# DRAM weight sums issued one per job, and 512-wide output products over half the inputs, in a two-layer mLSTM and GLA decoder kernel

## The chip, the cores and the metric

The kernel runs on one core of a Trainium2 chip. The metric is the time of one execution on the device in microseconds (us). Engines are named as in the profile: PE (TensorE matmuls), PEld (its weight loads), DVE (VectorE), ACT (ScalarE), POOL (GpSimd) and SP (SyncE, whose queue issues most DMAs).

## What is computed

Two layers over 512 tokens of width 1024, each `x <- x + RMSNorm(mixer(RMSNorm(x)))`. Layer 0 is an mLSTM mixer, layer 1 a gated linear attention (GLA). The parts that the change touches:

```python
uz = h @ w_in;  u, z = uz[..., :2048], uz[..., 2048:]      # layer 0
uc = silu(causal_conv(u))
q, k = uc_head @ wq, uc_head @ wk;  v = u_head @ wv        # 4 heads of 512
gates = q @ wg_q + k @ wg_k + v @ wg_v + b_gate            # 8 gates per token
hh = mlstm(q, k / sqrt(512), v, log_i, log_f)
y = (headnorm(hh) * norm_w + skip * uc) * silu(z)
out = y @ w_out                                            # 2048 -> 1024
...
v = h1 @ g_w_in[:, 2048:4096]                              # layer 1, the v projection
```

## The kernel before

Everything is float32, and each large product is made of three float32r matmuls: operands are split into a high part (ACT, line 138) and a low part (DVE, line 139), and high times high, high times low and low times high are added up in PSUM. Weights come in chunks of 128 x 1024 (512 KB): SP loads a chunk into one of three `raw` buffers (line 155), ACT makes `whi`, DVE makes `wlo`, in four buffers each.

The program is a list of jobs in a fixed order, most of which consume one chunk. `run_jobs` goes through the list: before a job it splits the chunks of the next three jobs (`LA`), then runs what earlier jobs put off (`later`), then as many entries of `steps` and `spare` as the job names, and then the job itself. Every engine executes its instructions in the order in which this program writes them.

Layer 0 works head by head. For each head there are four u jobs (`u_job`: 24 matmuls 512 wide, then the splitting of u and the convolution on ACT and DVE), two v jobs (`v_job`), two q jobs and two k jobs (`qk_job`). After the first u jobs of heads 1 to 3 the scores of the head before are made. The gate products of v (`v_gate`, lines 395 to 398) are put off in `spare` and made on DVE, POOL and ACT a few per job, from rows of weights (`wv`, line 390) that SP loads; their sum (`v_gates_end`, line 409) feeds the gacc matmuls behind head 3's score. The gate products of q and k are gacc matmuls at line 378, which read an ACT copy of q (line 541).

Layer 1's v projection is a Strassen-like product of 7 instead of 8 blocks, and needs sums of weight blocks. These sums (`vws`: U, W, Z and R, four tiles of 512 KB each) are made in DRAM by DMAs that POOL issues: 16 plain copies (`vws_start`, line 516) and 16 accumulating ones (`vws_add`, line 520). In the kernel before, each q and k job of heads 1 to 3 issues the next three of the 32, as long as there are any. Layer 1 reads the sums at about 690 us.

The output product of layer 0 has eight blocks of 128 features, two halves of the inputs (8 tiles of y each, `c` = 0 and 1; the second one holds heads 2 and 3) and two halves of the tokens. The first `NF` = 3 blocks take their first half of the inputs in `out_full` jobs: one chunk, with the token halves one after the other, 256 wide. Two of these jobs run before the last head's attention, and the third one has the last head's normalisation (`mid`, which is `head_steps`) between its token halves. For the other blocks `out_job` loads the chunk of `c` = 0 once for each token half. Blocks 3 and 4 take their `c` = 0 jobs of half 0 ahead of the second halves of the inputs. All are 256 wide.

When the first job of token half 1 is done, `after_half0` queues the residual step of half 0: the norm's factor, and then six `add` steps with an empty step after each, one step per job. `add` scales block pairs, adds the residual, and splits the result for layer 1 (`x1_done`, lines 927 to 930). The first norm matmul of layer 1 (`pre_rstd`) follows behind the last output job and needs all of them.

Of the kernel before, what the change touches and what calls it, by code (L numbers as in the profile page):

```python
# [9 lines left out]
F32 = mybir.dt.float32  # L10
# [3 lines left out]
ALU = mybir.AluOpType  # L14
AX = mybir.AxisListType

P = 128
# [79 lines left out]
def tile_mlstm_gla(ctx, tc, xT, pvec, cst, wg, wgv, w_min, w_qk, w_v, w_mout,  # L97
                   w_gqk, w_gr, w_gu, w_gv, w_gz, w_gout, pw, lvl_masks, out):
    nc = tc.nc
# [18 lines left out]
    def psum(name):  # L118
        return pp.tile([P, T], F32, tag="ps", bufs=8, name=name)

    def mm(out, lhsT, rhs, start, stop, more=False):

        nc.tensor.matmul(out, lhsT=lhsT, rhs=rhs, start=start, stop=stop, skip_group_check=more)  # L123
# [26 lines left out]
    def later(k, fn):  # L150
        laters.append([k, fn])
# [158 lines left out]
        eng.tensor_add(acc[:, sl], acc[:, sl], sq[:, sl])  # L310
        return acc

    def proj(ps, chunk, rhi, rlo, start=True, stop=True, sl=FULL):
        whi, wlo = chunk
        n = len(rhi)
        for k in range(n):
            wh, wl = part(whi, k * P, P), part(wlo, k * P, P)
            mm(ps, wh, rhi[k][:, sl], start and k == 0, False)
            mm(ps, wh, rlo[k][:, sl], False, False)
            mm(ps, wl, rhi[k][:, sl], False, stop and k == n - 1)  # L320

    def natural(pss, chunk, base, lhi, llo, total):
        whi, wlo = chunk
# [83 lines left out]
    def v_gates_end():  # L407
        for h in range(1, NH):
            nc.vector.tensor_add(vg[:, 0], vg[:, 0], vg[:, h])
        for i in range(4):  # L410
            mm(gacc[0:8, i * P:(i + 1) * P], vg[:, 0, i, :], ident, False, i == 3)

    A = [None] * NH
    V = [None] * NH
    st = {}
# [6 lines left out]
    def u_conv(n, src):  # L422
        c = t2("conv")
        nc.scalar.activation(c, src, AF.Identity, bias=col(PV_CB + n), scale=col(PV_CW + 48 + n))  # L424
        for j in range(1, 4):
            nc.vector.scalar_tensor_tensor(c[:, j:], src[:, 0:T - j], col(PV_CW + 16 * (3 - j) + n),  # L426
                                           c[:, j:], op0=ALU.mult, op1=ALU.add)

        def act():
            uc = t2("uc")  # L430
            use(SILU)
            nc.scalar.activation(uc, c, AF.Silu)
            ch[n], cl[n] = t2("chi", F32R), t2("clo", F32R)
            split(ch[n], cl[n], uc)
            us = t2("us")
            nc.scalar.mul(us, uc, col(PV_SKIP + n))
            nc.sync.dma_start(uc_d[n], us)

        later(1, act)
# [16 lines left out]
    def u_job(n):  # L456
        def run(chunk):
            ps = psum("u")
            if n < 4:
                proj(ps, chunk, ghi, glo)  # L460
                fps.append(ps)
            else:
                proj(ps, chunk, hhi, hlo)
                u_split(n, ps)
                u_conv(n, ps)
            if n == 2:
                acc = None
                for k in range(KD):
                    acc = add_square(acc, xt[k])
                st["accx"] = acc  # L470
            if n == 3:
                st["rsx"] = rstd_of([st["accx"]], D)
                u_scaled(range(4), fps)
                steps.extend([lambda k=k: h_step((k, k + 1)) for k in range(0, KD, 2)])

        job(run, ring(w_min[n]), b=3, la=1 if n == 2 else LA)
# [10 lines left out]
    def v_evac(h, pss):  # L487
        V[h] = t2s(f"V{h}", 4)
        for i in range(4):
            nc.scalar.activation(V[h][i], pss[i], AF.Copy, accum_out=vmean[:, 4 * h + i:4 * h + i + 1])  # L490
        c = vmean[:, 4 * h:4 * h + 4]
        nc.vector.tensor_scalar_mul(c, c, -1.0 / T)
        if h < NH - 1:
            for i in range(4):
                nc.sync.dma_start(v_d[4 * h + i], V[h][i])
        v_gates(h)

    def v_job(h, c):
        def run(chunk):
            if c == 0:  # L500
                st["v"] = [psum("v") for _ in range(4)]
            pss = st["v"]
            natural(pss, chunk, 2 * c, [uh[4 * h + i] for i in range(4)], [ul[4 * h + i] for i in range(4)], 4)
            if c == 1:
                later(1, lambda: v_evac(h, pss))

        job(run, ring(w_v[2 * h + c]), n=1, b=4)

    q32 = {}


    vws = {(n, p, c): dp.tile([P, 1024], F32, name=f"vw{n}{p}{c}") for n in "UWZR" for p in range(2) for c in range(2)}

    def vws_start(n, p, c):
        a11, a12, a21 = w_gv[2 * p, c], w_gv[2 * p, 2 + c], w_gv[2 * p + 1, c]
        nc.gpsimd.dma_start(vws[n, p, c], {"U": a21, "W": a11, "Z": a12, "R": a11}[n])

    def vws_add(n, p, c):
        a21, a22 = w_gv[2 * p + 1, c], w_gv[2 * p + 1, 2 + c]
        nc.gpsimd.dma_start(vws[n, p, c], {"U": a22, "W": vws["U", p, c], "Z": vws["W", p, c], "R": a21}[n],  # L520
                            accum_op=ALU.add, max_dma_last_dim=4096)

    vsums = [lambda n=n, p=p, c=c, f=f: f(n, p, c) for f in (vws_start, vws_add) for n in "URWZ"
             for p in range(2) for c in range(2)]

    def qk_job(h, which, c):
        d = (q, kq)[which]

        def run(chunk):
            whi, wlo = chunk  # L530
            for e in range(2):
                n = 4 * h + 2 * c + e
                ps = psum("qk")
                for k in range(4):
                    wh, wl = part(whi, k * 256 + e * P, P), part(wlo, k * 256 + e * P, P)
                    mm(ps, wh, ch[4 * h + k], k == 0, False)
                    mm(ps, wh, cl[4 * h + k], False, False)
                    mm(ps, wl, ch[4 * h + k], False, k == 3)
                d[n] = t2("qkh", F32R), t2("qkl", F32R)
                q32[n] = t2("q32")  # L540
                nc.scalar.copy(q32[n], ps)
                split(*d[n], ps)

            if c:
                parts = [(wgs[:, 16 * which + n, :], q32.pop(n)) for n in range(4 * h, 4 * h + 4)]
                later(2 if h else 3, lambda: gate_add(parts))
            if h:
                for f in [vsums.pop(0) for _ in range(min(3, len(vsums)))]:
                    f()

        job(run, ring(w_qk[which, 2 * h + c]), n=1, b=(1, 4, 4, 6)[h])

# [18 lines left out]
    def z_job(n=1, b=0, early=False):  # L571
        i = znext[0]
        znext[0] += 1

        def run(chunk):
            ps = psum("z")
            proj(ps, chunk, *((ghi, glo) if early else (hhi, hlo)))

            def evac():
                zs[i] = t2(f"z{i}")  # L580
                if early:
                    nc.vector.tensor_mul(zs[i], ps, st["rsx"])
                else:
                    nc.scalar.copy(zs[i], ps)
                raw_z.append(i)

            later(1, evac)

        job(run, ring(w_min[16 + i]), n=n, b=b)
# [230 lines left out]

    OUT = {}

    NF = 3

    KP = KD // 2

# [4 lines left out]
    def out_full(n, mid=None):  # L831

        def run(chunk):
            for half in range(2):
                OUT["ps", n, half] = psum("op")[:, HALF[half]]
                proj(OUT["ps", n, half], chunk, yhi[0:8], ylo[0:8], True, False, HALF[half])
                if mid and half == 0:
                    mid()

        job(run, ring(w_mout[2 * n]))  # L840

    def out_job(n, c, half, after=None):

        sl = HALF[half]

        def run(chunk):
            r = slice(8 * c, 8 * c + 8)
            if c == 0:
                OUT["ps", n, half] = psum("op")[:, sl]
            ps = OUT["ps", n, half]  # L850
            assert c == 0 or all(yhi[r])
            proj(ps, chunk, yhi[r], ylo[r], c == 0, c == 1, sl)
            if c == 1:
                if n % 2 == 0:
                    OUT["o", half, n // 2] = t2("o")
                OUT["acc", half] = add_square(OUT["acc", half] if n else None, ps, sl)
                nc.scalar.mul(pair(OUT["o", half, n // 2])[:, n % 2, :], ps, col(PV_POST + n))
            if after:
                after()

        job(run, ring(w_mout[2 * n + c]))
# [86 lines left out]
    def after_half0():  # L948
        rstd, add = residual(0)
        steps.append(rstd)  # L950
        for k in range(KP + 2):
            steps.extend([lambda k=k: add(k), lambda: None])

    rstdB, addB = residual(1)

    out_stage(lambda: (head_steps(NH - 1), steps.extend([lambda: None] * 4 + [lambda i=i: gla_weights(i // 2, i % 2) for i in range(4)])),
              after_half0, 2, 2)

# [379 lines left out]
        job(run, ring(w_gz[n]), la=la)  # L1340

    job(lambda: nc.vector.reduce_max(mx, nref, axis=AX.X), n=0)
    gz_job(0)
    job(lambda: (range_test(), gscale(0, 7), gscale(1, 7)))
    gz_job(1)
# [332 lines left out]
```

## Time and profile before

| | |
|---|---|
| median of 3 runs | 910.5 us (909.35 to 911.77) |
| profiled execution | 915.67 us |
| its span in the trace | 914.0 us |
| PE busy in the span | 892.4 us (98%) |
| DVE, ACT, POOL busy | 672.2, 559.9, 208.3 us |
| mean granted clock of PE | 0.994 of full |
| chunk loads for the output product of layer 0 | 29 |

The span is the time from the first to the last recorded instruction of the profiled execution; 1.67 us of that execution lie around it. Busy times count an engine's instructions as the trace has them. Matmuls overlap in PE's pipeline, so that the duration of one is longer than the step from one start to the next.

### The profile page before, as it was taken

To read this page: it belongs to the slowest core of one execution; us is meant where nothing else is said; L and a number is where in the kernel's file an instruction comes from. 1 tells how busy PE (TensorE), PEld (TensorE's weight loads), DVE (VectorE), ACT (ScalarE), POOL (GpSimd) and SP (SyncE) were. 2 spreads that over 40 slices of the span, in tenths; PEclk is the share of its full clock that TensorE was granted. 3 is DMA by queue.
4 is the path that set the end of the run, shared out by engine and by line. 5 is a ranking of instruction groups with operands and counts; after the bars stand their busy time and mean duration, and the time that the engine had idled before them with its cause. 6 is when DMAs were issued, how large, how long until landed. Compare 5 with 4: busy or idle time off the path is not lost. (4 is left out here: it accounts for less than half of the span.)

```text
span 914.0 us, 12691 instructions
## 1 busy us (share of the span) xinstructions
PE 892.4 (98%) x4576; PEld 746.7 (82%) x4576; DVE 672.2 (74%) x978; ACT 559.9 (61%) x953; POOL 208.3 (23%) x211
## 2 busy tenths in 40 slices
PE   9999999999998999999999999999999999999995
PEld 6887876778876788899999998777778888888884
DVE  5899796789796568878758764853786676778974
ACT  6866684775873558756666554546556555655762
POOL 0013563366170031445001130322000001201001
PEclk9999999999999999999999999999999999999998
DMA  8354488479797334223576696798277959976846
GB/s 304 122 171 134 132 278 286 137 231 259 226 221 216 104 127 138 89 74 115 180 225 207 206 292 229 190 245 211 93 257 251 306 185 328 301 268 216 278 142 138
DMA packets 63492, 185.34 MB, mean 203 GB/s; under 512 B 7392, under 2 KB 11872, under 8 KB 62880
## 3 DMA queue, kind: packets, MB, share of 16 engines
q1 hardware_dynamic: 52320, 137.07, 44.9%
q0 software_dynamic: 10816, 47.19, 20.0%
q8 instruction: 37, 0.61, 0.3%
q10 hardware_dynamic: 288, 0.22, 0.1%
q14 instruction: 31, 0.25, 0.1%
HBM read 160.33 MB, written 58.72 MB: 240 GB/s over the span
## 5 line engine op out<-in xcount | busy, mean ns | idle before, releaser
L139 DVE TENSOR_TENSOR wlo<-raw,whi 128x1024 fp32r<-128x1024 f32 (+1 forms) x158 | 205.9, 1314 | 83.4 <-ACT whi L138 82.2
L138 ACT CAST whi<-raw 128x1024 fp32r<-128x1024 f32 (+1 forms) x158 | 162.5, 1040 | 85.6 <-DMA raw<-in_w_min 26.6
L395 POOL TENSOR_TENSOR vp<-V,wv 128x512 f32<-128x512 f32 x56 | 87.4, 1652 | 165.3 <-ACT V L490 86.3
L123 PE MATMUL op<-yhi,whi 128*128 128x256 f32 x256 | 73.5, 287 | 0.0
L123 PE MATMUL op<-yhi,wlo 128*128 128x256 f32 x256 | 72.5, 283 | 0.4 <-DVE wlo L139 0.4
L123 PE MATMUL op<-ylo,whi 128*128 128x256 f32 x256 | 72.8, 284 | 0.0
L398 DVE SCALAR_TENSOR_TENSOR vp<-V,wv 128x512 f32<-128x512 f32 x72 | 69.2, 1000 | 3.2 <-DMA wv<-in_wgv 3.2
L123 PE MATMUL gz<-g2h,whi 128*128 128x512 f32 x128 | 51.2, 400 | 1.1 <-PEq L1301 1.1
L123 PE MATMUL qk<-chi,whi 128*128 128x512 f32 x128 | 50.2, 392 | 0.0
L123 PE MATMUL qk<-clo,whi 128*128 128x512 f32 x128 | 50.0, 390 | 0.2 <-DVE clo L139 0.2
L123 PE MATMUL gz<-g2h,wlo 128*128 128x512 f32 x128 | 50.0, 390 | 0.0
L123 PEld LDWEIGHTS op<-ylo,whi 128*128 128x128 f32 x256 | 49.1, 192 | 1.1 <-DVE ylo L139 0.6
L123 PE MATMUL qk<-chi,wlo 128*128 128x512 f32 x128 | 49.9, 390 | 0.0
L123 PE MATMUL gz<-g2l,whi 128*128 128x512 f32 x128 | 49.8, 389 | 0.0
L123 PEld LDWEIGHTS op<-yhi,wlo 128*128 128x128 f32 x256 | 49.1, 192 | 0.6 <-DVE wlo L139 0.6
L123 PEld LDWEIGHTS op<-yhi,whi 128*128 128x128 f32 x256 | 49.1, 192 | 0.5 <-issue 0.5
L123 PE MATMUL z<-hhi,whi 128*128 128x512 f32 x112 | 44.7, 399 | 0.0
L123 PE MATMUL z<-hlo,whi 128*128 128x512 f32 x112 | 44.4, 397 | 0.0
L123 PE MATMUL z<-hhi,wlo 128*128 128x512 f32 x112 | 44.2, 395 | 0.0
L426 DVE SCALAR_TENSOR_TENSOR conv<-u,pv,conv 128x511 f32<-128x511 f32 (+2 forms) x48 | 35.8, 748 | 11.3 <-ACT conv L424 10.2
L738 POOL TENSOR_TENSOR sq<-sq 128x512 f32<-128x512 f32 x12 | 17.6, 1470 | 108.2 <-ACT sq L736 107.9
L1254 POOL DMA_DIRECT2D gvhi<-gv_d x8 | 4.3, 543 | 147.3 <-DMA wpP<-klo 119.9
(320 smaller groups left out, 2606.6 us busy)
## 6 DMA issues: line engine op xcount, KB each, us to landing
raw<-in_w_min SPq DMA_DIRECT2D x30, 512.0 KB, 4.4
raw<-in_w_mout SPq DMA_DIRECT2D x29, 512.0 KB, 4.1
wv<-in_wgv SPq DMA_DIRECT2D x32, 256.0 KB, 5.8
raw<-in_w_qk SPq DMA_DIRECT2D x16, 512.0 KB, 4.3
raw<-in_w_gqk SPq DMA_DIRECT2D x16, 512.0 KB, 4.0
raw<-in_w_gz SPq DMA_DIRECT2D x16, 512.0 KB, 7.4
raw<-in_w_gv SPq DMA_DIRECT2D x12, 512.0 KB, 4.2
raw<-in_w_v SPq DMA_DIRECT2D x8, 512.0 KB, 7.4
```

The lines of the kernel that those rows point to most:

```text
L123: nc.tensor.matmul(out, lhsT=lhsT, rhs=rhs, start=start, stop=stop, skip_group_check=more)
L138: nc.scalar.copy(hi, src)
L139: nc.vector.tensor_sub(lo, src, hi.bitcast(F32))
L395: nc.gpsimd.tensor_mul(j, V[h][i], w)
L398: nc.vector.scalar_tensor_tensor(j, V[h][i], 1.0, w, op0=ALU.mult, op1=ALU.mult, accum_out=o)
L426: nc.vector.scalar_tensor_tensor(c[:, j:], src[:, 0:T - j], col(PV_CW + 16 * (3 - j) + n), c[:, j:], op0=ALU.mult, op1=ALU.add)
L738: nc.gpsimd.tensor_add(sqs[0], sqs[0], sqs[vt])
L1254: nc.gpsimd.dma_start(VS[h][i][r], gv_d[8 * (h - 2) + 4 * i + r])
```

## The change

The 32 DMAs of the weight sums are issued one at a time: one behind each u job from block 4 on (12), one behind each v job and each q or k job of heads 1 to 3 (6 and 12), and one behind the evacuation of each z job until the list is empty (the last 2). Their definitions move ahead of the u jobs. A line further down fails at build time if any is left.

`NF` becomes 5, and `out_full` makes both token halves at once, with 512-wide matmuls into one PSUM bank; `mid` now runs after the fourth of its eight input tiles. `out_job` for these blocks adds to one half of that bank at a time. The two `c` = 0 jobs of half 0 that ran ahead (`ahead` = 2) are gone, so blocks 0 to 4 each load the chunk of their first half of the inputs once, and the stage has 27 chunks. In `after_half0` the empty steps behind the last four `add` steps are dropped.

```diff
-    def proj(ps, chunk, rhi, rlo, start=True, stop=True, sl=FULL):
+    def proj(ps, chunk, rhi, rlo, start=True, stop=True, sl=FULL, more=False):
...
+    def vsum_next():
+        if vsums:
+            vsums.pop(0)()
...
                 u_split(n, ps)
                 u_conv(n, ps)
+                vsum_next()
...
             if c == 1:
                 later(1, lambda: v_evac(h, pss))
+            if h:
+                vsum_next()
...
             if h:
-                for f in [vsums.pop(0) for _ in range(min(3, len(vsums)))]:
-                    f()
+                vsum_next()
...
                 raw_z.append(i)
+                if not early:
+                    vsum_next()
...
-    NF = 3
+    NF = 5
...
         def run(chunk):
+            ps = psum("op")
             for half in range(2):
-                OUT["ps", n, half] = psum("op")[:, HALF[half]]
-                proj(OUT["ps", n, half], chunk, yhi[0:8], ylo[0:8], True, False, HALF[half])
-                if mid and half == 0:
+                OUT["ps", n, half] = ps[:, HALF[half]]
+            whi, wlo = chunk
+            for k in range(8):
+                wh, wl = part(whi, k * P, P), part(wlo, k * P, P)
+                mm(ps, wh, yhi[k], k == 0, False)
+                mm(ps, wh, ylo[k], False, False)
+                mm(ps, wl, yhi[k], False, k == 7)
+                if mid and k == 3:
                     mid()
...
-            proj(ps, chunk, yhi[r], ylo[r], c == 0, c == 1, sl)
+            proj(ps, chunk, yhi[r], ylo[r], c == 0, c == 1, sl, n < NF)
...
         for k in range(KP + 2):
-            steps.extend([lambda k=k: add(k), lambda: None])
+            steps.extend([lambda k=k: add(k)] + [lambda: None] * (k < 2))
...
-              after_half0, 2, 2)
+              after_half0, 2, 0)
```

## Rows read from the trace of the kernel before

**Rows 1.** The page's busy line: busy us, share of the span, instructions
```profile
PE 892.4 (98%) x4576; PEld 746.7 (82%) x4576; DVE 672.2 (74%) x978; ACT 559.9 (61%) x953; POOL 208.3 (23%) x211
```

**Rows 2.** Windows by stage: us, busy us (instructions) by engine, clock, DMA share, GB/s
```profile
74.74:105.47 30.73, 30.73 (x156) 25.30 (x153) 26.34 (x39) 19.44 (x38) 14.94 (x11) 1.00 0.43 131
105.47:149.12 43.65, 42.33 (x185) 31.68 (x183) 36.17 (x53) 30.29 (x69) 26.27 (x25) 1.00 0.82 274
149.12:185.54 36.42, 35.54 (x170) 29.61 (x169) 25.71 (x40) 24.01 (x50) 8.93 (x6) 1.00 0.48 161
...
215.78:250.75 34.97, 34.97 (x172) 29.75 (x169) 27.57 (x43) 25.94 (x54) 9.39 (x7) 1.00 0.83 238
250.75:301.15 50.40, 47.36 (x222) 36.23 (x220) 38.88 (x71) 28.56 (x60) 18.17 (x17) 0.97 0.80 211
...
471.29:506.06 34.77, 34.77 (x291) 34.67 (x289) 27.05 (x35) 23.07 (x41) 4.94 (x3) 1.00 0.66 211
...
494.40:506.06 11.66, 11.66 (x100) 11.59 (x98) 11.66 (x15) 8.05 (x15) 4.75 (x3) 1.00 0.56 178
```

**Rows 3.** Timeline of PE: start us, us, instruction, [idle before <-releaser]
```profile
144.84 1.03 PE L378 MATMUL gacc<-q,wgs 128*8 128x512 f32 x4
...
149.12 0.50 PE L123 MATMUL u<-hhi,whi 128*128 128x512 f32 x1
...
181.15 0.39 PE L123 MATMUL v<-whi,ulo 128*128 128x512 f32 x1
182.41 0.50 PE L123 MATMUL v<-whi,uhi 128*128 128x512 f32 x1 [0.88 <-ACT uhi L138]
...
202.72 1.04 PE L378 MATMUL gacc<-q,wgs 128*8 128x512 f32 x8
...
287.78 0.28 PE L123 MATMUL sc<-qkh,qkl 128*128 128x128 f32 x1
291.10 1.04 PE L123 MATMUL gacc<-cs,vg 128*8 128x128 f32 x8 [3.04 <-DVE vg L409]
292.06 0.64 PE L123 MATMUL z<-hhi,whi 128*128 128x512 f32 x1
...
295.48 0.49 PE L123 MATMUL z<-hhi,wlo 128*128 128x512 f32 x1
```

**Rows 4.** Timeline of ACT at the end of head 1
```profile
144.39 1.05 ACT L138 CAST whi<-raw 128x1024 fp32r<-128x1024 f32 x1 [10.45 <-DMA raw<-in_w_min]
```

**Rows 5.** Timeline of DVE, head 3's q and k jobs and behind
```profile
259.79 5.68 DVE L139 TENSOR_TENSOR wlo<-raw,whi 128x1024 fp32r<-128x1024 f32 x1
...
268.42 2.56 DVE L139 TENSOR_TENSOR wlo<-raw,whi 128x1024 fp32r<-128x1024 f32 x1
...
278.38 0.69 DVE L398 SCALAR_TENSOR_TENSOR vp<-V,wv 128x512 f32<-128x512 f32 x1 [1.40 <-DMA wv<-in_wgv]
...
287.53 0.69 DVE L398 SCALAR_TENSOR_TENSOR vp<-V,wv 128x512 f32<-128x512 f32 x1 [1.83 <-DMA wv<-in_wgv]
```

**Rows 6.** DMA issues, 118 to 150 us, then 74 to 116: KB each, median us to landing
```profile
raw<-in_w_min SPq DMA_DIRECT2D x3, 512.0 KB, 18.3
...
raw<-in_w_qk SPq DMA_DIRECT2D x4, 512.0 KB, 4.2
```

**Rows 7.** Groups of instructions on POOL: busy us, mean ns of one, idle before
```profile
L520 POOL DMA_DIRECT2D vwR<-in_w_gv x4 | 7.1, 3204 | 0.0
...
L516 POOL DMA_DIRECT2D vwU<-in_w_gv x4 | 2.3, 580 | 0.0
```

**Rows 8.** The chain in order of time, the 512-wide products of layer 1
```profile
837.23 43.81 PE op L123 x192
```

**Rows 9.** Tile raw, 60 to 310 us: ns min/median/max, first and last start
```profile
L139 DVE TENSOR_TENSOR wlo<-raw,whi x37: 1206/1218/5676, 59.7 to 309.5; 128x1024 fp32r<-128x1024 f32 x37
```

**Rows 10.** Waits of PE: us in total, times, longest
```profile
PE op L123 <- DVE wlo L139: 0.4, 1, 0.4
```

**Rows 11.** Timeline of POOL before the seam to layer 1
```profile
504.71 1.29 POOL L310 TENSOR_TENSOR sq<-sq 128x512 f32<-128x512 f32 x1 [3.86 <-PE op L123]
```

More of the change, by code (lines that the diff above doesn't have):

```diff
@@ L317, in proj @@
             wh, wl = part(whi, k * P, P), part(wlo, k * P, P)
-            mm(ps, wh, rhi[k][:, sl], start and k == 0, False)
-            mm(ps, wh, rlo[k][:, sl], False, False)
-            mm(ps, wl, rhi[k][:, sl], False, stop and k == n - 1)
+            mm(ps, wh, rhi[k][:, sl], start and k == 0, False, more)
+            mm(ps, wh, rlo[k][:, sl], False, False, more)
+            mm(ps, wl, rhi[k][:, sl], False, stop and k == n - 1, more)
     def natural(pss, chunk, base, lhi, llo, total):
@@ L411, in v_gates_end, with vws_start, vws_add @@
             mm(gacc[0:8, i * P:(i + 1) * P], vg[:, 0, i, :], ident, False, i == 3)
+    vws = {(n, p, c): dp.tile([P, 1024], F32, name=f"vw{n}{p}{c}") for n in "UWZR" for p in range(2) for c in range(2)}
+    def vws_start(n, p, c):
+        a11, a12, a21 = w_gv[2 * p, c], w_gv[2 * p, 2 + c], w_gv[2 * p + 1, c]
+        nc.gpsimd.dma_start(vws[n, p, c], {"U": a21, "W": a11, "Z": a12, "R": a11}[n])
+    def vws_add(n, p, c):
+        a21, a22 = w_gv[2 * p + 1, c], w_gv[2 * p + 1, 2 + c]
+        nc.gpsimd.dma_start(vws[n, p, c], {"U": a22, "W": vws["U", p, c], "Z": vws["W", p, c], "R": a21}[n],
+                            accum_op=ALU.add, max_dma_last_dim=4096)
+    def vsum_next():
+        if vsums:
+            vsums.pop(0)()
+    vsums = [lambda n=n, p=p, c=c, f=f: f(n, p, c) for f in (vws_start, vws_add) for n in "URWZ"
+             for p in range(2) for c in range(2)]
     A = [None] * NH
@@ L505, in run @@
                 later(1, lambda: v_evac(h, pss))
+            if h:
+                vsum_next()
         job(run, ring(w_v[2 * h + c]), n=1, b=4)
     q32 = {}
[L512 to L524, printed above, removed]
     def qk_job(h, which, c):
@@ L1342, in tile_mlstm_gla @@
     job(lambda: nc.vector.reduce_max(mx, nref, axis=AX.X), n=0)
+    job(lambda: vsums and 1 / 0, n=0)
     gz_job(0)
```

## The prediction

> **What bounds the kernel now.** I read the page's busy line first [rows 1]: TensorE (PE) is busy 98% of the 914.0 us span, the next engine, VectorE (DVE), 74%. So only two things shorten this kernel: fewer or cheaper matmuls, or the gaps of PE. The page adds that PE's busy time is modelled, so I looked for gaps in the start times instead: wherever the next matmul starts later than the one before it needs, the difference is lost time. The largest losses after the start lie in layer 0, where this change works. The windows by stage [rows 2] say how loaded the other engines and the DMA engines are there; the timelines of PE, ScalarE (ACT) and DVE [rows 3 to 5] say who was late.
>
> Three places in layer 0 matter. First, eight small gacc matmuls that belong to head 1 start at 144.84, and the next stage's u matmul only at 149.12 [rows 3]. Eight of the same kind at 202.72 take 1.04 us altogether, so 3.2 to 3.3 us are lost. PE waited for the q copy of ACT, and ACT had stood still for 10.45 us for a chunk of weights, up to 144.39 [rows 4]. The DMA answer shows why [rows 6]: in that stretch raw chunks took 18.3 us from issue to landing, beside the twelve transfers of 512 KB that GpSimd (POOL) issues in head 1, three to a q or k job; before the burst the same kind of chunk took 4.2 us. The DMA engines are at 0.82 over the whole stage from 105 to 149 us, against 0.43 in the stage before it [rows 2].
>
> Second, at 181.15 a v matmul waits for the last uhi split: 182.41 minus 181.15 minus 0.23 is 1.0 us [rows 3]. ACT and DVE come into this stage late from the first stall, so I read it as an echo. Third, at 287.78 PE runs dry until 291.10 (3.2 us lost) because the v gates are not yet summed, and then runs at half clock: the matmuls from 292.06 to 295.48 come 0.43 us apart instead of 0.23, eight of them, 1.6 us more. Together 4.8 us. DVE was late there twice over: it waited 1.40 and 1.83 us for wv rows, and one weight split, at 259.79, took 5.68 us where the median is 1.22, in the stretch in which POOL issues accumulating transfers and multiplies [rows 5, 9].
>
> **The transfers, part by part.** Nothing is added or removed: 16 plain and 16 accumulating issues before and after. They move from 11 q and k jobs, three at a time, to 12 u, 6 v, 12 q/k and 2 z jobs, one at a time. A job is about 5.5 us long (24 matmuls at 228 ns, below).
>
> The price of one issue on POOL is 0.58 us for a plain one and up to 3.2 us for an accumulating one in the burst [rows 7]; POOL is busy a quarter to three quarters of these stages [rows 2], and nothing on PE waits for POOL but the v gates' sum at 291. The first sums are read only in layer 1, some 400 us later, so their landing is free. What is queued behind an issue on POOL is the next v-gate product; the DMA queue of SyncE gets nothing new.
>
> What goes: the burst of twelve. With one transfer in 5.5 us a raw chunk shares the DMA engines with at most one or two others. I bound its landing by 4.2 us (alone) and 18.3 us (beside twelve) [rows 6]; three raw buffers at 5.5 us a job hide some 16 us. I take it as hidden: the 3.3 us go (bounds 0 and 3.3). Of the echo at 181 I take 0.8 us (bounds 0 and 1.0). For the v gates, head 3 will still see ten accumulating issues, but one per job, so a split that is held for 4.5 us, and the SyncE queue that waits behind it for a free raw buffer, should be rarer: I take 3.6 of 4.8 us (bounds 0 and 4.8).
>
> What comes instead: issues now fall into the u jobs, where DVE is busiest: 26.3 of 30.7 us in head 1's, 25.7 of 36.4 in head 2's, 27.6 of 35.0 in head 3's [rows 2]. They hold DVE: two held splits cost 1.35 and 4.47 us over their 1.21 [rows 5, 9]. Four issues to a stage at 1.35 us are 5.4 us, against idle DVE time of 4.4, 10.7 and 7.4 us, so head 1 would be late by 1.0 us. Plain issues, which are all that heads 1 and 2 have in their u jobs, are shorter than the accumulating ones of those two rows, so I take 0.3 us (bounds 0 and the rival below).
>
> The Trainium skill ("SBUF — State Buffer", section "SBUF: two separate sides") speaks against putting these issues beside a busy DVE: the port pair that DVE and GpSimd share is an exclusive lock held for the whole instruction, and the later one is blocked until the first ends. By that rule an issue would hold DVE for no more than its own length; at the 0.58 us row head 1 would not be late at all and the sum would be 0.3 us better, while at the 3.2 us row the same rule leads to the rival below. The trace agrees that DVE operations stretch beside POOL's, but not with the bound: 4.47 us were lost in one split, across several POOL instructions.
>
> **The output products.** Blocks 3 and 4 of the first half of the inputs go from 2 x 24 matmuls 256 wide to 24 at 512, and so they are loaded and split once instead of twice. Blocks 0 to 2 already shared one load, and go from 48 at 256 to 24 at 512. So five times 48 become five times 24. The stage from 471.29 to 506.06 holds 288 matmuls 256 wide by the code: 120.7 ns each; weight loads are busy 34.67 of its 34.77 us, so narrower products cannot go faster [rows 2]. At 512 wide 192 matmuls took 43.81 us: 228.2 ns each [rows 8]. Per pair 241.4 minus 228.2 is 13.2 ns; 120 pairs give 1.6 us, and with single steps of 120 ns 1.4. I take 1.5 us.
>
> The Trainium skill ("TensorE: Matmul & The Clock Gate", section "Back-to-back issue gap") gives 262 cycles for 256 columns and 518 for 512, so a pair would gain 6 cycles and 120 pairs an estimated 0.3 us instead of 1.5. The rows do not bear it out, their steps are longer at both widths; the rows decide.
>
> Two loads and splits fewer save DVE and ACT 2.4 and 2.1 us, worth nothing on PE by themselves. Between the last head's normalisation and the first product that needs it there now lie 2.9 + 11.0 us instead of 2.9 + 5.8, so PE's wait of 0.4 us for wlo there [rows 10] goes: 0.4 (bounds 0 and 0.6, with the pipe's refilling).
>
> **The seam to layer 1.** The stage's second half now has 10 jobs behind the point at which the residual of half 0 is queued, not 12; to fit, the empty steps behind the last four additions are dropped. Four additions then come one per 2.9 us job, where they came one per two jobs. DVE was already full there, 11.66 of 11.66 us [rows 2], and POOL's last sum of squares ended at 504.71 + 1.29 = 506.00 [rows 11], just before the stage's end at 506.06, where the norm's matmul follows that needs it: no slack. For it: the last addition now stands one job before the end, not at it. Below it costs nothing; above, a step takes some 5.3 us of DVE's rhythm with two weight splits or 4.1 with one, four take 16.4 us, the five jobs from the first of them to the end last 14.4, and POOL's sum comes behind: 3.4 us. I take 0.8.
>
> **The sum.** 3.3 + 0.8 + 3.6 + 1.5 + 0.4 - 0.3 - 0.8 = 8.5 us. The profiled execution took 915.67 us (914.0 and 1.67 around it), so it would take 907.2. The timed runs have a median of 910.5, 5.2 us less than the profiled one. Some of those 5.2 us may be these very waits, longer under the profiler: all of it would leave 3.3 us of gain (907.2), none of it 8.5 (902.0). I take 6.8, nearer to the second since the DMA queues are the same without a profiler: 903.7 us. All bounds at their best give 1.6 + 0.6 + 3.3 + 1.0 + 4.8 = 11.3 us, 899.2.
>
> **The other ways.** A measurement of this kernel tells about 0.3% (2.7 us) from no change.
>
> (a) The waits go, as summed: 903.7 us, 900 to 907. Chance 0.60.
>
> (b) The v-gate wait before the first z jobs stays, since DVE has 32 gate products of head 3 to do in any case: 903.7 + 3.6 = 907.3. For it: DVE is at 38.9 of 50.4 us there with few gaps [rows 2]. Against: the two waits for wv and the held split are 7.7 us. Chance 0.10.
>
> (c) The dense residual steps make PE wait at the seam: 903.7 + 3.4 - 0.8 = 906.3, or 908 if the norm waits behind a late load too. Chance 0.12.
>
> (d) The transfers' spreading does nothing, because timed runs don't have these waits or the chunks come late for another reason: 1.9 us of products remain, less the seam's 0.8: about 909.4. Against it: eighteen us to landing in the burst. Chance 0.12.
>
> (e) On the other side: POOL's issues in the u jobs hold DVE so long that uhi and ulo of each head come late and the v jobs wait. With x us per issue, four to a stage, heads 1 to 3 lose what is above 4.4, 10.7 and 7.4 us; at x = 2.55 that is 5.8 + 0 + 2.8 = 8.6, which eats the sum. At the 3.2 us row [rows 7] it is 8.4 + 2.1 + 5.4 = 15.9 us in place of the 0.3 taken: 919.3. For it: the 5.68 us split. Against: heads 1 and 2 have plain issues in their u jobs. Chance 0.06.
>
> Faster by over 0.3% (below 907.8): (a), (b) and half of (c), 0.76. Within: half of (c) and (d), 0.18. Slower: (e), 0.06. The range reaches from the best bounds less some of the runs' own scatter (they lie 2.4 us apart), 898.5, to (d), 909.5; it leaves out (e) and little more.
>
> **What would show it.** Right: no ACT wait of 10 us for raw in head 1, gacc at its end in 1 us, raw chunks landing in under 10 us from 105 to 280 us, PE at full clock around 290, 512-wide op matmuls 228 ns apart, and 27 chunks loaded for the output products. Wrong: a wait of v for uhi or ulo in any head; ACT or DVE waiting for raw or wv in the u jobs; PE waiting for vg as before; the norm's matmul before the first gqk starting more than 1 us after the last op. The prediction fails most easily on the v-gate term, whose chain has three links that the spreading only eases.

## The result and the profile after

The changed kernel takes 906.57 us (906.34 to 907.64, five runs) against 911.47 us (909.35 to 913.09, five runs) for the kernel before: a ratio of 0.9941, with a 95% interval of 0.9916 to 0.9965. Measured again on another chip it was 906.35 against 911.71 us, 0.9944 (0.9923 to 0.9964). So it is faster by 0.6%, 4.9 and 5.4 us. The ratios and their intervals are those on record, formed from the runs; they differ from the quotients of the two medians by up to 0.0015. The profiled execution took 906.34 us, with a span of 904.6 us; that of the kernel before took 915.67 us. The two traces are therefore 9.3 us apart, twice as far as the medians, and this has to be explained too.

The windows by stage of the changed kernel follow [as rows 2; the columns are the same].

```profile
73.67:104.41 30.74, 30.74 (x157) 25.30 (x153) 26.33 (x39) 19.38 (x38) 13.52 (x13) 1.00 0.59 185
104.41:146.97 42.56, 41.15 (x186) 31.36 (x184) 39.93 (x54) 33.27 (x75) 25.89 (x23) 1.00 0.83 273
146.97:181.94 34.97, 34.97 (x172) 29.77 (x169) 27.20 (x42) 24.20 (x48) 9.01 (x9) 1.00 0.63 203
...
211.41:246.38 34.97, 34.97 (x172) 29.76 (x169) 25.14 (x37) 24.36 (x48) 10.34 (x9) 1.00 0.82 205
246.38:293.69 47.31, 46.03 (x221) 34.98 (x219) 37.94 (x70) 28.24 (x59) 16.41 (x15) 1.00 0.71 185
...
467.33:497.27 29.94, 29.14 (x243) 28.91 (x241) 23.39 (x31) 21.62 (x41) 5.75 (x3) 1.00 0.62 196
```

The first number of a row, the length of its stage, is what to read first. Head 1's v, q and k jobs with the first u job behind them took 43.65 us and take 42.56; head 2's u and v jobs fell from 36.42 to 34.97, with PE busy all the time; the stage from head 3's q jobs through the gates fell from 50.40 to 47.31, and its clock is 1.00 where it was 0.97 [rows 2]. The DMA share of the stage of head 1's v, q and k jobs has hardly moved, 0.82 to 0.83. What moved is who waits. In the DMA answer for 118 to 150 us (KB each, median us to landing) raw chunks land in 5.9 us where they took 18.3 [rows 6]:

```profile
raw<-in_w_min SPq DMA_DIRECT2D x4, 512.0 KB, 5.9
vwW<-in_w_gv POOLq DMA_DIRECT2D x4, 512.0 KB, 4.8
```

The timeline of PE has the places of [rows 3] and two more:

```profile
112.79 0.39 PE L123 MATMUL v<-wlo,uhi 128*128 128x512 f32 x1
114.36 0.50 PE L123 MATMUL v<-whi,ulo 128*128 128x512 f32 x1 [1.18 <-DVE ulo L139]
...
145.99 1.04 PE L378 MATMUL gacc<-q,wgs 128*8 128x512 f32 x8
146.97 0.50 PE L123 MATMUL u<-hhi,whi 128*128 128x512 f32 x1
...
283.71 0.28 PE L123 MATMUL sc<-qkh,qkl 128*128 128x128 f32 x1
285.24 1.04 PE L123 MATMUL gacc<-cs,vg 128*8 128x128 f32 x8 [1.25 <-DVE vg L409]
286.21 0.50 PE L123 MATMUL z<-hhi,whi 128*128 128x512 f32 x1
286.55 0.40 PE L123 MATMUL z<-hlo,whi 128*128 128x512 f32 x1
...
417.94 1.13 PE L123 MATMUL ssq<-sq,cs 128*128 128x512 f32 x2 [0.55 <-POOL sq L746]
...
497.27 1.13 PE L123 MATMUL ssq<-sq,cs 128*128 128x256 f32 x4 [0.80 <-POOL sq L310]
```

The eight gacc matmuls of head 1 now pass in one piece, and the next u matmul comes 0.98 us behind their start instead of 4.28. The wait for the v gates is 1.4 us instead of 3.2 (285.24 minus 283.71, less one step), and the z matmuls behind it run at full clock. A v matmul of head 1 waits, which it did not do before: 114.36 minus 112.79 minus 0.23 is 1.3 us. Two norms wait for POOL, 0.55 and 0.80 us. For the first of them these are POOL's rows, in the kernel before and in the changed one:

```profile
420.08 5.31 POOL L738 TENSOR_TENSOR sq<-sq 128x512 f32<-128x512 f32 x3 [14.84 <-ACT sq L736]
412.60 5.28 POOL L746 TENSOR_TENSOR sq<-sq 128x512 f32<-128x512 f32 x3 [14.85 <-ACT sq L744]
```

To set executions against each other I take three stretches from the starts in the timelines of PE: the heads (from the first v matmul to the first fps matmul), the output (from the first op matmul of layer 0 to rc in layer 1), and the time to the end.

| profiled execution | heads, us | output, us | execution, us | median of timed runs, us |
|---|---|---|---|---|
| before | 258.3 | 143.3 | 915.67 | 911.47 |
| before, second profile | 258.6 | 143.6 | 918.48 | 915.50 |
| changed | 251.9 | 141.8 | 906.34 | 906.57 |
| changed, second profile | 251.8 | 141.8 | 905.45 | 906.35 |

The trace thus gives 6.4 us to the heads, where the transfers were spread, and 1.5 us to the output, 7.9 us together (6.8 and 1.9 between the two second profiles). The stretches between them agree within 0.1 us from the first fps to the first op. The rest of the difference lies where the change does nothing: the first v matmul starts at 40.0 to 41.0 us in these four executions, and layer 1 from rc to the end of the span takes 367.4 to 371.7 us, longest in the second profile of before.

### The profile page after: what moved, and what is told of

The parts are those of the page before. It is cut to its first block, busy times and chain, and to the rows that moved or that the text cites. A ratio compares the mean times of both kernels' runs of the same rounds, so it can differ in the third digit from the quotient of the medians.

```text
span 904.6 us, 12439 instructions
## 1 busy us (share of the span) xinstructions
PE 885.6 (98%) x4456; PEld 739.6 (82%) x4456; DVE 670.5 (74%) x976; ACT 559.3 (62%) x951; POOL 205.2 (23%) x211
## 5 line engine op out<-in xcount | busy, mean ns | idle before, releaser
L139 DVE TENSOR_TENSOR wlo<-raw,whi 128x1024 fp32r<-128x1024 f32 (+1 forms) x156 | 209.7, 1353 | 77.0 <-ACT whi L138 75.5
L395 POOL TENSOR_TENSOR vp<-V,wv 128x512 f32<-128x512 f32 x56 | 80.8, 1493 | 164.5 <-ACT V L510 70.8
L123 PE MATMUL op<-yhi,whi 128*128 128x256 f32 (+1 forms) x216 | 66.4, 308 | 0.0
L123 PE MATMUL op<-ylo,whi 128*128 128x256 f32 (+1 forms) x216 | 65.4, 303 | 0.0
L123 PE MATMUL op<-yhi,wlo 128*128 128x256 f32 (+1 forms) x216 | 65.4, 303 | 0.0
L398 DVE SCALAR_TENSOR_TENSOR vp<-V,wv 128x512 f32<-128x512 f32 x72 | 63.0, 915 | 1.9 <-DMA wv<-in_wgv 1.9
L123 PEld LDWEIGHTS op<-yhi,whi 128*128 128x128 f32 x216 | 41.3, 191 | 2.0 <-issue 0.5
L123 PEld LDWEIGHTS op<-ylo,whi 128*128 128x128 f32 x216 | 41.3, 191 | 2.0 <-issue 0.5
L123 PEld LDWEIGHTS op<-yhi,wlo 128*128 128x128 f32 x216 | 41.3, 191 | 1.6
L123 PE MATMUL u<-hhi,whi 128*128 128x512 f32 x96 | 37.8, 394 | 0.0
```

What stands on the lines that cost most here:

```text
L139: nc.vector.tensor_sub(lo, src, hi.bitcast(F32))
L395: nc.gpsimd.tensor_mul(j, V[h][i], w)
L398: nc.vector.scalar_tensor_tensor(j, V[h][i], 1.0, w, op0=ALU.mult, op1=ALU.mult, accum_out=o)
```

## Experiments

Each kernel was timed beside the kernel before on the same chip. The chips differ in the time of the kernel before (911.4 to 915.5 us), so ratios are compared across chips, not times.

### The kernel before, profiled again

Nothing is edited.

> The kernel before, unchanged, profiled a second time. Its first profiled execution took 915.67 us while five timed runs lie at 909.35 to 913.09. If the three waits (3.3 us at the end of head 1, 1.0 us in head 2's v jobs, 4.8 us at the v gates) vary from execution to execution, this one shows them shorter or missing by some 2 to 5 us in all and takes 910 to 913 us. If they are the same in each execution and only the first profile had something else that was slow, the three come out within 0.5 us of the first profile.

It took 918.48 us. ACT again waited 10.6 us for raw at the end of head 1, and PE again lost 3.4 us at gacc and 3.4 us at the v gates (for these two the first profile has 3.3 and 3.2); the v wait of head 2 was missing, so that one is not fixed. The half clock behind the gates lasted longer: from 284 to 300 us the clock was 0.79 on the mean (columns as in rows 2), where the first profile has 0.89.

```profile
284.00:300.00 16.00, 12.78 (x58) 9.40 (x57) 6.61 (x16) 5.59 (x11) 0.00 (x0) 0.79 0.44 162
```

So the two main waits are there in every profile of this kernel and their size varies little; what varies is what follows from them. The execution is also 3 us above the median of the timed runs of its chip, as the first one was 4.2 us above its own; but the 23 timed runs on that chip reach from 911.56 to 919.16 us, so 918.48 us lies among them, while the first profile's 915.67 us lies above all five of its own (913.09 us at most).

### The products alone

```diff
-                vsum_next()                  # in u, v and z jobs
...
             if h:
-                vsum_next()
+                for f in [vsums.pop(0) for _ in range(min(3, len(vsums)))]:
+                    f()                      # in q and k jobs, as before
```

> Only the output products and the denser residual steps are changed; the 32 transfers stay three to a q or k job. By the prediction's terms it gains 1.5 + 0.4 - 0.8 = 1.1 us on the kernel before: ratio about 0.9988. Rival: the products carry most of the 4.9 us measured for the whole change: ratio 0.995 or below.

912.53 against 915.50 us, a ratio of 0.9975 (0.9954 to 0.9996). The trace has 258.4 us for the heads and 141.8 for the output: nothing and 1.8 us against the second profile of before. The expected 1.1 us lies in the interval; the rival's 0.995 lies just outside it, and the heads have not moved. The wait of 0.80 us for POOL at the seam is here too.

### The transfers alone

```diff
-    NF = 5
+    NF = 3
...
-            steps.extend([lambda k=k: add(k)] + [lambda: None] * (k < 2))
+            steps.extend([lambda k=k: add(k), lambda: None])
```

with `out_full` and the two jobs that run ahead as they were.

> Only the 32 transfers are spread, one behind each job; the output products and the residual steps are those of the kernel before. If the transfers carry the change, it gains what is left of 4.9 us, 3.8 us: ratio about 0.996, with no ACT wait of 10 us for raw in head 1 and gacc there in 1.0 us, and a new wait of v for ulo of 1 to 2 us in head 1. If the products carry it: ratio 0.999 to 1.000.

909.88 against 915.50 us, 0.9946 (0.9929 to 0.9964). The heads take 252.6 us, the output 143.4. ACT's wait for raw in head 1 is 0.8 us, and the new v wait of head 1 is there with 1.4 us. There is no wait for POOL at the seam. The transfers carry the change: about two parts of three by the medians (5.6 us beside the 3.0 of the products alone), three of four by the trace (6.0 beside 1.8).

The two ratios multiplied give 0.992, where the whole change was measured at 0.9941 and 0.9944. Before the second measurement of the whole I had expected 0.992 if the two halves add up and 0.994 to 0.995 if they overlap. The times speak for some overlap, but the intervals of the halves are too wide to show one, and in the trace the two act in different stretches.

### The burst put back in head 1

```diff
                 u_conv(n, ps)
-                vsum_next()
+                if n >= 8:
+                    vsum_next()
...
-            if h:
+            if h > 1:
                 vsum_next()                  # v jobs
...
             if h:
-                vsum_next()
+                for _ in range(3 if h == 1 else 1):
+                    vsum_next()              # q and k jobs
```

> The changed kernel, but in head 1 the u and v jobs issue none of the transfers and the four q and k jobs three each, so that the burst of twelve comes back there alone; heads 2 and 3 stay at one a job. If the burst is what made raw chunks late, ACT again waits about 10 us for raw at the end of head 1, PE loses 3.3 us at gacc, the echo in head 2's v jobs comes back with 1.0 us, and head 1's own v wait (1.8 us, new in the changed kernel) goes: 2.5 us slower than the changed kernel's 906.6, about 909. If the chunks were late for another reason, raw lands in under 8 us there and the time is 905 to 907.

907.82 against 915.50 us, 0.9925 (0.9895 to 0.9954): no slower than the changed kernel, so the price that I expected was not paid. The cause came back all the same. Among ACT's waits from 110 to 155 us (total, times, longest) raw is first again:

```profile
ACT whi L138 <- DMA raw<-in_w_min: 11.0, 2, 7.7
```

In the changed kernel this row reads 0.3 us. But of 7.7 us PE saw only 0.5 at gacc, as its timeline shows (the step is 1.53 us, of which 0.98 is the time without a wait):

```profile
143.74 1.61 PE L378 MATMUL gacc<-q,wgs 128*8 128x512 f32 x8
145.27 0.50 PE L123 MATMUL u<-hhi,whi 128*128 128x512 f32 x1
```

With 9.4 us (the products alone) PE lost 2.2, with 9.8 (the moved gates' step, below) 2.7, with 10.4 and 10.6 us (before, twice) 3.3 and 3.4. In all five traces the loss is ACT's wait less 7.1 to 7.2 us: that much of the wait costs PE nothing, and what lies above it costs one for one, as far as these waits reach. The v wait of head 1 went, as expected, and one of 0.8 us came in head 2.

The trace of this run does not say "no slower", though: its heads take 254.2 us, 2.3 more than in the changed kernel, and the execution took 909.73 us. That is about what I expected, but its parts are not. Up to head 3's u jobs only 0.3 us have come together, and the rest lies at the v gates: PE waits 1.76 us for them instead of 1.42, 0.2 us are lost in the score ahead of them, and the half clock comes back (1.5 us more from the start of gacc to fps). The timed runs scatter from 905.33 to 912.42 us; whether the slower ones among them are those with the half clock is not shown.

### The gates' step moved behind a z job

```diff
     z_job(b=16)
     job(lambda: (gates0(), score(NH - 1)))
+    z_job()
     job(gates1)
-    job(silu_z, n=0)
-    z_job()
     job(silu_z, n=0)
```

in the kernel before; one of two `silu_z` jobs goes with the move.

> The kernel before with one thing moved: the step that sums the v gates and feeds the gacc matmuls stands behind the next z job, not ahead of it, so PE has 5.5 us of other work while DVE ends the gate products. Transfers and products are those of before. If the v-gate wait and the half clock behind it are a main part of what the spreading of the transfers gained, this alone gains their 4.8 us and more: ratio 0.9925 to 0.995, no PE wait for vg, full clock from 284 to 300. If PE just waits somewhere later for the same late DVE, or these waits are not in timed runs: 0.998 to 1.000.

911.14 against 911.71 us, 0.9999 (0.9981 to 1.0016): nothing. The wait only moved. The next step reads a DVE copy of the same sums, and in the waits of PE (total, times, longest) it stands first:

```profile
PE fps L123 <- DVE gs L633: 3.1, 1, 3.1
```

The half clock stayed as well (0.89 on the mean from 284 to 300 us, as before). So a job in between buys no time when its neighbour depends on the same engine; it is DVE that has to be earlier.

### All transfers out of the heads

```diff
-                vsum_next()                  # in u, v, q and k jobs
...
                 if not early:
+                    vsum_next()
                     vsum_next()              # z jobs
...
                 if mid and k == 3:
                     mid()
+            vsum_next()                      # out_full jobs
```

> The changed kernel with all 32 transfers out of the heads' jobs: two behind each z job from the first late one on and one behind each 512-wide output job, where the DMA engines were at 0.34. If what is left in layer 0 (1.84 us at the v and q jobs of head 1, 1.4 us at the v gates) comes from POOL's issues and the transfers, both go: 2 to 3 us below the changed kernel, unless POOL's squares and skip products, which the z jobs' heads need, are now late. If they come from the gate products on POOL and DVE themselves, they stay and the time is that of the changed kernel within 1 us.

902.04 us (899.60 to 903.52) against 911.71 us, 0.9891 (0.9865 to 0.9916). The changed kernel on the same chip has 0.9944 (0.9923 to 0.9964), so the step beyond it is clear. The heads take 248.1 us. These are all waits of PE in its trace that the answer lists (total, times, longest):

```profile
PE warm L123 <- DVE warm L289: 1.6, 1, 1.6
PE gz L123 <- PEq L1312: 1.3, 1, 1.3
PE ssq L123 <- POOL sq L310: 0.8, 1, 0.8
PE gv L123 <- DVE wlo L139: 0.6, 1, 0.6
PE op L123 <- DVE o L1523: 0.3, 1, 0.3
PE gv L123 <- DVE vf L1246: 0.3, 1, 0.3
```

Nothing is left in the heads: the waits for ulo, for clo, for vg and for the q copy are gone, and so is the wait of the last head's norm for POOL. DVE has the v gates summed by 279.3 us (three additions from 278.57 on take 0.72 us), and PE comes to them at 281.40. The gate products are the same, so by themselves they were not the cause.

### The empty steps placed elsewhere

```diff
-            steps.extend([lambda k=k: add(k)] + [lambda: None] * (k < 2))
+            steps.extend([lambda k=k: add(k)] + [lambda: None] * (k in (2, 3)))
```

> The changed kernel with the two empty steps that are left put behind the third and the fourth addition in place of the first and the second, so that the last four additions have two more jobs between them and the first ones are dense. If the density of the last four makes POOL's last sum late, PE's wait of 0.8 us for it at the seam goes and the time falls by 0.8 to 1.0 us (0.1%, at the edge of what five rounds can tell, so the trace decides). If POOL is late for the place of the last addition itself, the wait stays.

907.72 against 911.71 us, 0.9941 (0.9913 to 0.9970): not to be told from the changed kernel's 0.9944 by time. In the trace the wait of the ssq matmul for POOL's line 310 is gone, and the output takes 140.7 us instead of 141.8, 1.0 us less. The density made POOL late: the wait is 0.8 us in all six traces with four dense additions at the end, and 0.2 us at most in the seven with empty steps among them.

### The plain transfers from SyncE's queue

```diff
-        nc.gpsimd.dma_start(vws[n, p, c], {"U": a21, "W": a11, "Z": a12, "R": a11}[n])
+        nc.sync.dma_start(vws[n, p, c], {"U": a21, "W": a11, "Z": a12, "R": a11}[n])
```

> The changed kernel with the 16 plain transfers issued from SyncE's queue instead of POOL's, at the same places in the program; the 16 accumulating ones stay with POOL. The DMA traffic of heads 1 and 2 stays, POOL's issues in their u jobs go. If POOL's issues (0.54 us each, and the shift that they give to POOL's gate products) make DVE late in head 1, the waits of v and q there (1.8 us in the first trace, 1.3 us in the second) go: 905 or a little below. If the traffic makes them, they stay and the time is that of the changed kernel, 906 to 907, or worse, because the raw loads now queue behind these issues.

904.43 against 911.36 us, 0.9922 (0.9895 to 0.9948), by time not to be told from the changed kernel's 0.9944; in the trace the heads take 250.2 us, 1.7 less than in the changed kernel, and no v or q matmul of heads 1 to 3 waits any more. The traffic is the same, so POOL's issues caused that wait; the wait for the v gates (1.4 us) stays, so the plain issues did not cause that one. How they did it shows in the timeline of DVE in head 1. First the changed kernel:

```profile
106.11 2.23 DVE L139 TENSOR_TENSOR wlo<-raw,whi 128x1024 fp32r<-128x1024 f32 x1
108.45 1.59 DVE L139 TENSOR_TENSOR clo<-uc,chi 128x512 fp32r<-128x512 f32 x1
109.96 3.13 DVE L398 SCALAR_TENSOR_TENSOR vp<-V,wv 128x512 f32<-128x512 f32 x1
```

then the same three with the plain transfers on SyncE's queue:

```profile
106.56 1.22 DVE L139 TENSOR_TENSOR wlo<-raw,whi 128x1024 fp32r<-128x1024 f32 x1
108.91 0.69 DVE L139 TENSOR_TENSOR clo<-uc,chi 128x512 fp32r<-128x512 f32 x1 [1.13 <-ACT chi L138]
109.52 0.68 DVE L398 SCALAR_TENSOR_TENSOR vp<-V,wv 128x512 f32<-128x512 f32 x1
```

and POOL's timeline in the changed kernel:

```profile
105.96 3.52 POOL L395 TENSOR_TENSOR vp<-V,wv 128x512 f32<-128x512 f32 x2 [7.22 <-DVE conv L445]
109.44 0.54 POOL L418 DMA_DIRECT2D vwR<-in_w_gv  x1
109.99 2.54 POOL L395 TENSOR_TENSOR vp<-V,wv 128x512 f32<-128x512 f32 x2
```

The three DVE operations lose 1.01, 0.90 and 2.45 us. No issue of 0.54 us is as long as the last loss; it is as long as the two gate products of POOL from 109.99 to 112.53. With the plain transfers on SyncE's queue all four products run earlier and in one piece, and are over before DVE's own gate products begin:

```profile
102.48 6.46 POOL L395 TENSOR_TENSOR vp<-V,wv 128x512 f32<-128x512 f32 x4 [3.74 <-DVE wlo L139]
```

Of the shift only 0.54 us is the issue between the two pairs. The first pair starts 3.5 us later in the changed kernel, released by a convolution of DVE and not by a weight split, and so it does in the three other traces with plain issues in head 1's u jobs (at 105.8 to 106.7 us); in the eight traces of the other kernels without such issues the four products start at 102.1 to 103.0 us, and no v matmul of head 1 waits. So the place of POOL's products is what costs DVE; why an issue in the u jobs moves the first pair by so much is not shown.

### Both at once

The edits of the two experiments "All transfers out of the heads" and "The empty steps placed elsewhere" together.

> Both at once: the transfers in the late z jobs and output jobs, and the two empty steps behind the third and the fourth addition. The first alone gave 902.0 us (ratio 0.9891), the second took the 0.8 us wait at the seam out of the trace: about 901.2, ratio 0.988. If the denser first additions cost what the last ones gain, 902.

902.87 against 911.36 us, 0.9905 (0.9879 to 0.9930). The output is down to 140.1 us in the trace, the heads stay at 248.1, but layer 1 took 1.4 us more than in the profile without the moved steps, with a wait of 1.3 us for vf (0.4 us at most in the others). By time it is not to be told from the version without the moved steps.

### The transfers out of the heads, products as before

```diff
-    NF = 5
+    NF = 3
...
                 if mid and half == 0:
                     mid()
+                vsum_next()                  # twice in each out_full job
```

with the rest of the output as before, and the transfers in the late z jobs.

> The kernel before with the 32 transfers moved to the late z jobs and the 256-wide output jobs; the output products and the residual steps are those of before. Beside the version that has both, this prices the products where the heads have no waits: by the steps of PE they are worth 1.5 us and the 0.4 us wait, less 0.8 us at the seam and 0.7 us at the last head's norm, so 0.4 us and up to 1.5: 902.5 to 903.5 (ratio 0.9895 to 0.991). If they are worth 2.3 us, as the products alone seemed to on the first chip: 904.3.

905.25 us (904.49 to 910.14) against 911.36 us, 0.9933 (0.9905 to 0.9961), outside the expected 902.5 to 903.5. Against the version with both edits on the same chip (902.52 to 904.01) the products are worth 905.25 minus 902.87, 2.4 us, and 3.4 by the trace (output 143.5 and 140.1 us). Neither of the two waits for POOL at the seam, so all of it is the products'. That is more than their steps and the wait of 0.4 us in [rows 10]. The start times in the kernel before show why. The splits of y and of the weights behind the last head's normalisation are late there over several matmuls (three of PE's weight loads wait 0.18 to 0.19 us each for ylo), and the row counts only the last of them:

```profile
436.47 0.28 PE L123 MATMUL op<-yhi,whi 128*128 128x256 f32 x1
...
439.52 0.39 PE L123 MATMUL op<-yhi,wlo 128*128 128x256 f32 x1 [0.40 <-DVE wlo L139]
439.74 0.28 PE L123 MATMUL op<-yhi,whi 128*128 128x256 f32 x1
```

These are 15 steps in 3.27 us where 15 of 0.12 would take 1.80: 1.5 us lost. The same loss stands in every trace with the products 256 wide (1.9 us here) and in none with 512. The heads take 248.1 us again, so nothing of the gain there comes from the products.

## Why the prediction was right

It gave 903.7 us, 898.5 to 909.5; the time is 906.57. The sign and the mechanism were right, and the largest terms. That the sum fits the trace so well (907.2 us for a profiled execution, which took 906.34) is in part luck: 1.4 of the 9.3 us lie in stretches that the change does not touch, and in the 7.9 us of the two others several terms that were off cancel. Of the signs of being wrong that it named, one came: a v matmul waits for ulo. The point forecast is 2.9 us low.

- **The burst in head 1, 3.3 us:** right. The next u matmul follows 0.98 us behind the start of gacc, where it took 4.28. That the burst makes the chunks late is shown by putting it back: ACT waits 7.7 us. That this costs PE 3.3 us holds for a wait of 10.45 us; by the five traces a wait of 7.1 us would have cost nothing.
- **The echo in head 2, 0.8 of 1.0 us:** gone in the changed kernel, and back with 0.8 us when the burst is put back, but also missing in the second profile of before. It depends on small shifts, and the term was luck.
- **The v gates, 3.6 of 4.8 us:** 1.8 us of the wait and 1.6 us of half clock went, 3.4 together. The reasons were right in kind: with the transfers out of the heads the wait is zero, and moving the step alone gives nothing. Whether the 1.4 us that stay come from the accumulating issues on POOL or from the traffic, no run tells.
- **Held DVE, 0.3 us:** this term was mis-sized. Head 1 lost 1.8 us in the first trace (1.3 at v, 0.5 at q) and 1.3 us in the second; the 0.5 at q stands in head 2 of the kernel before, so 1.3 and 0.8 us are new. I had priced an issue by its own length or by a held split of head 3, and took little because plain issues are short. The runs show that the harm comes with POOL's gate products standing where DVE's own operations run beside them and lose time. Even so the rival with its 15.9 us was far off; two heads did not wait.
- **The products, 1.5 and 0.4 us:** the first is right. The first two 512-wide jobs put 48 matmuls into 11.29 us (394.26 to 405.55), 0.4 us of it one late step: 227 ns each against 228.2 worked out. The second is mis-sized: the wait for wlo is gone, but with the late splits ahead of it it was 1.5 us and not 0.4. And 27 chunks are loaded.
- **The seam, 0.8 us:** the wait is 0.80 us by its row. That the four dense additions cause it is shown by the moved empty steps.
- **Not foreseen, 0.7 us:** the last head's norm waits for POOL's squares (line 746). I had written that nothing on PE waits for POOL but the gates' sum. By the two rows of POOL above, its three squares start 18.3 us behind the first op in both kernels (401.73 and 394.26). In the kernel before they ended at 425.39, 0.06 us ahead of the norm's matmul: there was no slack. With the jobs ahead of it 512 wide PE would get to the norm 0.75 us earlier (0.62 in the first two jobs, 0.13 in the half of the third), but ACT's squares, which POOL's follow, do not move, so this gain is lost again. Where the transfers are out of the heads, ACT's squares start 0.9 us earlier against the first op, and the wait is gone; how the two hang together is open.
- **The step to the median:** here are 1.9 of the 2.9 us; the other 1.0 is the median of before, 911.47 us from five runs where the forecast started from 910.5 from three. The traces gave 9.3 us, a little more than the sum; the medians 4.9 and 5.4. I had taken 6.8 between the two ends 3.3 and 8.5. The executions with a burst in head 1's q and k jobs ran above their medians under the profiler: before by 4.2 and 3.0 us, the one with the moved gates' step by 3.6, the products alone by 1.7, the burst in head 1 by 1.9. The others lie between 0.9 below and 1.3 above, the changed kernel 0.2 and 0.9 below. That the profiler makes such waits longer fits this. So does a plain variation from run to run: beside each other on one chip the timed runs of before reach over 7.3 us, those of the changed kernel over 3.7. No run tells the two apart, so this stays open.

The Trainium skill was cited against the change ("SBUF — State Buffer", section "SBUF: two separate sides"): an exclusive lock between DVE and GpSimd, held for the whole instruction. The trace agrees that one of the two holds the other up: one DVE product lost 2.45 us beside two POOL products of 2.54 us. It differs in the length, two POOL instructions and not one. What the prediction had wrong was to apply it to the issue instead of to the products.

Two readings of rows in the prediction were off without moving the sum: POOL's highest share in [rows 2] is 26.27 of 43.65 us, 60% and not three quarters, and what stands behind `mid` in its job is now 12 x 228 ns, 2.7 us and not 2.9.

## What to carry to other kernels

Background transfers belong where the DMA engines and the engine that issues them are less busy, and where what they push back has slack. With the same output products, spreading them through the busy stage came to 0.6% in all, and moving them to the stage of the z jobs (0.36 DMA share from 291.87 to 394.26 us in the changed kernel) and behind it to 1.1%. Price an issue by what moves on its engine and by who then runs beside that, not by its own duration. A wait in the rows can understate what a late engine costs: compare start times over the whole stretch. And when the profiled execution lies well above the timed runs, take the gain on a wait from the trace as an upper bound: here about half of it reached the median.

## What was not expected of the hardware

A late load was free for PE up to an ACT wait of 7.1 to 7.2 us, and cost it one for one beyond (7.7 us cost 0.5, 9.4 cost 2.2, 10.4 cost 3.3). An idle time of 3 us or more of PE at the gates was followed by matmuls 0.43 us apart instead of 0.23, the lower of the two clock levels, in each profile that had it. After 1.4 us there it was not, after 1.76 us it was (the run with the burst in head 1). But the length of the idle time alone does not decide: in the changed kernel PE stood still for 1.9 us in layer 1, from 631.54 to the next matmul, and went on at steps of 0.23 us.

```profile
631.54 0.39 PE L123 MATMUL gz<-g2h,wlo 128*128 128x512 f32 x1
633.65 0.47 PE L123 MATMUL gz<-g2h,whi 128*128 128x512 f32 x1 [1.72 <-PEq L1315]
633.95 0.39 PE L123 MATMUL gz<-g2l,whi 128*128 128x512 f32 x1
634.18 0.40 PE L123 MATMUL gz<-g2h,wlo 128*128 128x512 f32 x1
```

And a weight split on DVE, which has a median of 1.22 us, took up to 7.3 us in the changed kernel, longer than the 5.68 us of before, and 2.4 us at most without transfers in the heads.
